# A kernel's order of issue worked out by a list schedule and pinned, in place of the framework's own scheduler

## The chip, the cores and the metric

One core of a Trainium2 chip (trn2) runs the whole program. The metric is the device time of one execution in microseconds, the median of several runs. The engines are named PE or TensorE (matmuls and transposes), ACT or ScalarE, DVE or VectorE, POOL or GpSimd, and SP, whose queue issues the weight transfers.

## The reference

Two layers, each a half-step SwiGLU feed-forward net, a token mixer, and another half-step net, each between RMS norms. 256 tokens, width 1024, feed-forward width 2816, float32.

```python
for l in range(DEPTH):
    g = norm_g[l]
    h = swiglu_ffn(rmsnorm(x, g[0]), ffn_w_gate[l, 0], ffn_w_up[l, 0], ffn_w_down[l, 0])
    x = x + 0.5 * rmsnorm(h, g[1])
    h = hybrid_mixer(rmsnorm(x, g[2]), w_in[l], ..., w_out[l])
    x = x + rmsnorm(h, g[3])
    h = swiglu_ffn(rmsnorm(x, g[4]), ffn_w_gate[l, 1], ffn_w_up[l, 1], ffn_w_down[l, 1])
    x = x + 0.5 * rmsnorm(h, g[5])
```

`swiglu_ffn` is `(silu(h @ w_gate) * (h @ w_up)) @ w_down`. `hybrid_mixer` projects `h` by `w_in` into the inputs of three groups and multiplies their joined outputs by `w_out`: gated linear attention over chunks of 64 tokens (4 heads), a causal depthwise convolution of width 31 over 256 channels with layer norm and swish, and attention in a window of 128 tokens with 8 query heads, ALiBi and a sink per head.

## The kernel before

The 256 tokens are two tiles t of 128. Activations lie transposed as the stationary operand, weights stream past. A float32 product is made of three matmuls in the type fp32r (`mm3`, L183 to L186): each operand is split into a rounded `hi` and a rest `lo`. For the weights this is the work of `emit_unit` (L153): one DMA by SP into one of 4 `raw` buffers (L160), the cast `hi` on ScalarE (L164), the subtraction `lo` on VectorE (L170) or, for some of the mixer's units, GpSimd, each into one of 8 buffers. `done` releases a buffer once both token tiles have used it and emits the next unit.

A feed-forward net (`ffn`) goes over seven chunks of its 2816 columns, 384 or 512 wide: gate matmuls (into PSUM tiles `gu`), silu on ScalarE, up matmuls, the product `h` on VectorE, its transposes (L328), and the down matmuls of the chunk before (into `ga` and `sa`). `pre` (L262) makes a net's input: the norm's sum of squares (L259), transposes of `x` (L271), scaled evictions `xh` on ScalarE (L275) and the rest `xl` on VectorE (L279). It needs `gT`, the transposed norm weights (L190, L191). `post` (L285) is the norm of an output tile, added to `x`.

`late_setup` runs behind the gate matmuls of the second chunk of the first net: it loads constants over ScalarE's DMA queue. `tb` (L217) is loaded into one of two buffers `sc`, GpSimd makes the ALiBi table from it by eight operations (L219) and masks (L220), and only then has `ts` (L225) and after it `cwr`, the 31 + 1 rows of conv weights and bias (L228, L229), a buffer. TensorE transposes `cwr` (L235).

The mixer's pieces stand in a string (`SCRIPT`, L125): projections c, k, q, b, a of each tile, then queries and scores (S), their output (O), the gates (G, R), the linear attention (K, L, P, C), conv taps (T), the conv's end (Y, Z), the output projection (W) and the norm with the next net's input (A). A tap takes a product on ScalarE and a sum on GpSimd (L641, L642), or one operation on VectorE (L635). `kv_in` evicts the keys (`ts`, L680) for transposes (L685). `swa_q` evicts the queries (`sq`, L692), TensorE transposes them (L695), ScalarE evicts again (`qp`, L697). `swa_scores` makes scores (L711, L715), the sink's term (L718, L719), the negated maximum (L720) and the exponentials (L723), which `swa_out` transposes (L735) and multiplies with the values (L745).

The text of the program is not the order of issue. The framework's scheduler takes the traced instructions and, with its own cost model and the program's order as priority, sets each engine's order. `tc.issue_after` tells it not to put the setup and the mixer ahead of a named instruction.

Of the kernel before, what the change touches and what calls it, by code (L numbers as in the profile page):

```python
# [1 line left out]

# [12 lines left out]
PSUM = bass.MemoryType.PSUM  # L15
# [32 lines left out]
def trunk_kernel(  # L48
# [5 lines left out]
    nc = tc.nc  # L54
    V, G, A, PE = nc.vector, nc.gpsimd, nc.scalar, nc.tensor
# [10 lines left out]
    def nm(s):  # L66
        uid[0] += 1
        return f"{s}_{uid[0]}"
# [82 lines left out]
    state = {"emitted": 0, "released": 0, "m": 0}  # L151
# [47 lines left out]
    one = cp.tile([P, 1], F32, tag="one", name="one")  # L199
# [6 lines left out]
    def bcast(dst, src):  # L206
        A.dma_start(out=dst, in_=src.partition_broadcast(P))

    def late_setup():
# [52 lines left out]
    def pre(t, l, n):  # L262
        x = xs[t]
        r = rstd_of(sumsq([x[:, 0:512], x[:, 512:1024]])) if (t, l, n) != (0, 0, 0) else None
        hi = [ap.tile([P, P], F32R, tag=f"xh{t}_{k}", name=nm("xh")) for k in range(KT)]
        lo = [ap.tile([P, P], F32R, tag=f"xl{t}_{k}", name=nm("xl")) for k in range(KT)]
        for hf in range(2):
            ps = ps_tile("tr")
            for i in range(4):
                k = hf * 4 + i  # L270
                PE.transpose(out=ps[:, i * P:(i + 1) * P], in_=x[:, k * P:(k + 1) * P], identity=ident)  # L271
            for i in range(4):
                k = hf * 4 + i
# [137 lines left out]
        A.activation(out=out, in_=out, func=AF.Exp, scale=-1.0)  # L411

    def mixer(l, first, xT, after):
        with tc.issue_after(state["silu"].ins):
            ld = A.preload_act_table_set("natural_log_exp_and_others")
        with tc.issue_after(ld.ins):
            return mixer_body(l, first, xT, after)

    def mixer_body(l, first, xT, after):
        gng = mp.tile([P, 256], F32, tag="gng", name=nm("gng"))  # L420
        bcast(gng, gng_d[l].rearrange("h d -> (h d)"))
        lng = mp.tile([P, 256], F32, tag="lng", name=nm("lng"))
        bcast(lng, lng_d[l])
        lnb = mp.tile([P, 256], F32, tag="lnb", name=nm("lnb"))
        bcast(lnb, lnb_d[l])
        nr = {}

        def neg(t):
# [414 lines left out]
    xT[1]()  # L843


_INS = ['x', 'norm_g', 'ffn_w_gate', 'ffn_w_up', 'ffn_w_down', 'w_in', 'gla_w_gate2', 'gla_b_gate', 'gla_norm_g',
# [52 lines left out]
```

## Time and profile before

| what | value |
|---|---|
| median of 3 runs | 1011.09 us (1008.58 to 1011.55) |
| the profiled execution | 1012.63 us, its span 1010.6 us |
| mean granted clock of TensorE | 0.986 |
| TensorE busy | 969.1 us, 96% |
| VectorE, ScalarE, GpSimd busy | 592.4, 543.6, 133.9 us |
| read from memory | 169.88 MB, 169 GB/s over the span |

The page gives averages over the span. The stages differ: the four feed-forward nets, and the two mixers between them at about 206 to 330 and 696 to 822 us. So the views below are taken by stage. A granted clock of 1.00 is 2.4 GHz, one of 0.50 is 1.2 GHz. Idle time in brackets is that of the engine just before the row.

### The profile page before, as it was taken

Reading aid. Unit: us, or ns where it says so; the run is one execution under the profiler, and the core shown is the slowest. Engines: PE = TensorE matmul, PEld = TensorE weight load, DVE = VectorE, ACT = ScalarE, POOL = GpSimd, SP = SyncE. Lnnn points to the kernel's source line nnn. Section 1 sums busy time; section 2 is a strip of 40 time slices with the busy share of each in tenths; the row PEclk is TensorE's granted clock in tenths of the full one; section 3 lists DMA queues with packets and bytes.
Section 4 is the critical chain, followed back from the end, with each engine's and each line's share of the span. In section 5 each row is a group of like instructions: output and inputs, shape, how many; then the busy total and the mean of one; then the engine's idle time right before and its main releaser. Section 6 shows DMA issues by size and latency. Waiting matters only on the chain.

```text
span 1010.6 us, 13078 instructions
## 1 busy us (share of the span) xinstructions
PE 969.1 (96%) x4745; PEld 825.8 (82%) x4745; DVE 592.4 (59%) x894; ACT 543.6 (54%) x935; POOL 133.9 (13%) x158
## 2 busy tenths in 40 slices
PE   7959999998899999999999999999899999999997
PEld 7848888987688988888998888898787888888896
DVE  6634554567787764554576554456576886554453
ACT  7524443577885654443475444455778575444441
POOL 1110000027551000000000000000576110000000
PEclk9979999999999999999999999999989999999999
DMA  8846655734143676655648666564522348666541
GB/s 292 281 119 187 188 177 159 211 115 149 63 131 105 222 230 188 187 177 164 185 141 270 188 187 193 158 201 139 183 83 101 94 142 270 188 187 194 156 150 42
DMA packets 81971, 171.78 MB, mean 170 GB/s; under 512 B 5939, under 2 KB 29682, under 8 KB 81907
## 3 DMA queue, kind: packets, MB, share of 16 engines
q1 hardware_dynamic: 79952, 168.97, 53.9%
q10 hardware_dynamic: 1955, 1.98, 0.8%
q8 instruction: 37, 0.61, 0.2%
q14 instruction: 27, 0.22, 0.1%
HBM read 169.88 MB, written 1.05 MB: 169 GB/s over the span
## 4 chain that ended last, share of the span: by engine, by line
PE 79%; ACT 7%; DVE 4%; DMA 3%; POOL 3%; issue 2%; POOLq 0%; SPq 0%; ACTq 0%; DVEq 0%
PE gu L185 16%; PE gu L186 16%; PE gu L184 16%; PE ga L184 4%; PE ga L185 4%; PE ga L186 4%; PE sa L186 4%; PE sa L185 4%; PE sa L184 4%; PE tr L328 2%; ACT hi L164 2%; DVE lo L170 1%; ACT sc L723 1%; POOL cy L642 1%; DMA raw<-in_ffn_w_gate_dram 1%
## 5 line engine op out<-in xcount | busy, mean ns | idle before, releaser
L170 DVE TENSOR_TENSOR lo<-raw,hi 128x1024 fp32r<-128x1024 f32 (+3 forms) x316 | 369.4, 1174 | 309.2 <-ACT hi L164 308.3
L164 ACT CAST hi<-raw 128x1024 fp32r<-128x1024 f32 (+2 forms) x336 | 331.7, 995 | 371.9 <-PE gu L186 206.9
L185 PE MATMUL gu<-lo,xh 128*128 128x512 f32 (+2 forms) x864 | 326.1, 377 | 0.0
L184 PE MATMUL gu<-hi,xh 128*128 128x512 f32 (+2 forms) x864 | 326.0, 377 | 0.1
L186 PE MATMUL gu<-hi,xl 128*128 128x512 f32 (+2 forms) x864 | 324.8, 376 | 0.0
L185 PEld LDWEIGHTS gu<-lo,xh 128*128 128x128 f32 x864 | 163.7, 190 | 23.4 <-DVE lo L170 0.8
L184 PEld LDWEIGHTS gu<-hi,xh 128*128 128x128 f32 x864 | 163.6, 189 | 22.8 <-ACT sg L315 0.4
L186 PEld LDWEIGHTS gu<-hi,xl 128*128 128x128 f32 x864 | 163.8, 190 | 22.5
L252 POOL TENSOR_TENSOR rstd<-var,mhalf 128x1 f32<-128x1 f32 x24 | 13.1, 547 | 744.5 <-DVE var L251 744.5
L184 PE MATMUL ga<-hi,hh 128*128 128x512 f32 x176 | 69.4, 394 | 0.0
L185 PE MATMUL ga<-lo,hh 128*128 128x512 f32 x176 | 69.0, 392 | 0.0
L186 PE MATMUL ga<-hi,hl 128*128 128x512 f32 x176 | 68.9, 392 | 0.0
L186 PE MATMUL sa<-hi,hl 128*128 128x512 f32 x176 | 68.9, 391 | 0.0
L184 PE MATMUL sa<-hi,hh 128*128 128x512 f32 x176 | 68.8, 391 | 0.0
L185 PE MATMUL sa<-lo,hh 128*128 128x512 f32 x176 | 68.5, 389 | 0.0
L170 POOL TENSOR_TENSOR lo<-raw,hi 128x1024 fp32r<-128x1024 f32 (+1 forms) x20 | 47.0, 2354 | 34.8 <-ACT hi L164 34.8
L642 POOL TENSOR_TENSOR cy<-tc,cy 128x256 f32<-128x256 f32 x60 | 43.9, 732 | 15.4 <-ACT tc L641 11.7
L186 PEld LDWEIGHTS ga<-hi,hl 128*128 128x128 f32 x176 | 33.3, 189 | 7.1
L185 PEld LDWEIGHTS ga<-lo,hh 128*128 128x128 f32 x176 | 33.3, 189 | 6.6
L184 PEld LDWEIGHTS ga<-hi,hh 128*128 128x128 f32 x176 | 33.3, 189 | 6.6
L184 PEld LDWEIGHTS sa<-hi,hh 128*128 128x128 f32 x176 | 33.1, 188 | 6.9
L185 PEld LDWEIGHTS sa<-lo,hh 128*128 128x128 f32 x176 | 33.1, 188 | 6.9
(186 smaller groups left out, 997.7 us busy)
## 6 DMA issues: line engine op xcount, KB each, us to landing
raw<-in_ffn_w_down_dram SPq DMA_DIRECT2D x88, 512.0 KB, 3.4
raw<-in_ffn_w_gate_dram SPq DMA_DIRECT2D x64, 512.0 KB, 3.7
raw<-in_ffn_w_up_dram SPq DMA_DIRECT2D x64, 512.0 KB, 3.8
raw<-in_ffn_w_gate_dram SPq DMA_DIRECT2D x32, 384.0 KB, 3.3
raw<-in_ffn_w_up_dram SPq DMA_DIRECT2D x32, 384.0 KB, 3.3
raw<-in_w_in_dram SPq DMA_DIRECT2D x16, 512.0 KB, 5.5
raw<-in_w_out_dram SPq DMA_DIRECT2D x16, 512.0 KB, 3.8
raw<-in_w_in_dram SPq DMA_DIRECT2D x16, 392.0 KB, 3.9
```

The lines of the kernel that those rows point to most:

```text
L164: A.copy(out=hi[:, :n], in_=raw[:, :n])
L170: eng.tensor_tensor(out=lo[:, :n], in0=raw[:, :n], in1=hi[:, :n].bitcast(F32), op=ALU.subtract)
L184: PE.matmul(out=out, lhsT=xh, rhs=wh, start=start, stop=False)
L185: PE.matmul(out=out, lhsT=xh, rhs=wl, start=False, stop=False)
L186: PE.matmul(out=out, lhsT=xl, rhs=wh, start=False, stop=stop)
L252: G.tensor_tensor(out=r, in0=v, in1=mhalf[:, 0:1], op=ALU.pow)
L328: PE.transpose(out=ps[:, i * P:(i + 1) * P], in_=h[:, i * P:(i + 1) * P], identity=ident)
L642: G.tensor_tensor(out=yc, in0=m, in1=yc, op=ALU.add)
L723: A.activation(out=sc[:, h, :], in_=sc[:, h, :], func=AF.Exp, bias=mx[:, h:h + 1], accum_out=ls[:, h:h + 1])
```

## The change

No instruction is added, dropped or altered. When all instructions have been traced, `arrange` (new) gives each a cost, simulates the engines, and takes the instruction that can start first, the earlier one of the program at a tie. The order found is pinned on each engine by dependences without semaphores, and so is the order in which buffers are opened by different engines. The mixer's three broadcasts of norm weights, and the setup, keep their place behind a named instruction by `issue_after`, now the program's own.

```diff
+    held = []
+    @contextmanager
+    def issue_after(ins):
+        ...
     def late_setup():
-        with tc.issue_after(state["silu"].ins):
+        with issue_after(state["silu"].ins):
             late_setup_body()
...
     xT[1]()
+    arrange(tc, held)
...
+class Op:
+    def cost(self):
+        ...
+        if self.dma:
+            self.busy, self.after = (.37 if e == "SP" else .45), None
+        ...
+        elif e == "DVE":
+            ...
+                t = (.205 if op == "ISA" else .145) + .00105 * max(n, 1)
+        elif e == "Pool":
+            ...
+                t = .25 + .0019 * n if n > 8 else (.55 if n == 1 else 1.04)
+def order_of_issue(ops):
+    ...
+    for _ in range(n):
+        for e in engs:
+            if e not in known:
+                c = None
+                for k in ready[e]:
+                    when = room(ops[k])
+                    if when is None:
+                        continue
+                    when = max(when, free[e], at[k])
+                    if c is None or when < c[0] - 1e-9:
+                        c = (when, k)
+                        ...
+                known[e] = c
+        start, k = min(c for c in known.values() if c is not None)
+        o = ops[k]
+        end = start + (o.after or 0.)
+        if o.dma:
+            landed = end = max(start + 3.5, landed + o.bytes / 390e3)
+        ...
+def arrange(tc, held):
+    ...
+    out, first = order_of_issue(ops)
+    info = mybir.DependencyInfo(mybir.DependencyClass.NoSync, mybir.DependencyReason.DATA)
+    for e in ("PE", "Activation", "DVE", "Pool", "SP"):
+        for a, b in zip(out[e], out[e][1:]):
+            tc.add_manual_dep(b.i, a.i.name, info, reason="order of issue")
+    for b, a in first:
+        if a.eng != b.eng:
+            tc.add_manual_dep(b.i, a.i.name, info, reason="order of buffers")
```

By the new functions every line of the kernel from L209 on stands 7 or 8 lines further down.

**Place 1, the setup.** ScalarE, from the first cast behind the first DMAs of the setup, before (`hi` and `raw` are buffers of one weight unit):

```order
L164 CAST hi_552<-raw_551 128x1024
L164 CAST hi_572<-raw_571 128x1024
L225 DMA ts_522<-in_constants_dram 128x576
L228 DMA cwr<-in_conv_w_dram 31x2x256
L229 DMA cwr<-in_conv_b_dram 1x512
L164 CAST hi_590<-raw_589 128x1024
L164 CAST hi_608<-raw_607 128x1024
L164 CAST hi_626<-raw_625 128x1024
L164 CAST hi_648<-raw_647 128x1024
```

and now:

```order
L164 CAST hi_552<-raw_551 128x1024
L164 CAST hi_572<-raw_571 128x1024
L164 CAST hi_590<-raw_589 128x1024
L233 DMA ts_522<-in_constants_dram 128x576
L164 CAST hi_608<-raw_607 128x1024
L164 CAST hi_626<-raw_625 128x1024
L236 DMA cwr<-in_conv_w_dram 31x2x256
L237 DMA cwr<-in_conv_b_dram 1x512
L164 CAST hi_648<-raw_647 128x1024
```

The second `ts` DMA stands behind one more cast, the two `cwr` DMAs behind three more. TensorE at the transposes of `cwr`, in the middle of the up matmuls (`gu`) of the second chunk, before:

```order
L186 MATMUL gu_557<-hi_440,xl_112 128x512
L184 MATMUL gu_557<-hi_440,xh_105 128x512
L235 MATMUL tr_529<-cst,cwr 128x32 x4
L185 MATMUL gu_557<-lo_441,xh_105 128x512
L186 MATMUL gu_557<-hi_440,xl_113 128x512
```

and now, at the end of the first half of the down matmuls of the first chunk:

```order
L184 MATMUL sa_201<-hi_476,hh_421 128x512
L185 MATMUL sa_201<-lo_477,hh_421 128x512
L243 MATMUL tr_529<-cst,cwr 128x32 x4
L186 MATMUL sa_201<-hi_476,hl_422 128x512
L336 MATMUL tr_671<-cst,h_631 128x128 x4
L336 MATMUL tr_680<-cst,h_633 128x128 x4
```

Between the two places lie 31 matmuls. In the first microseconds, the copy of `gT` (L191) now stands behind the first two `lo` subtractions on VectorE, and a second weight cast and a sum of squares stand ahead of the first `xh` evictions on ScalarE.

**Place 2, mixer 1 on ScalarE, the queries of the second tile** (`sq_2250`, evicted from `gu_2201`; `tc` are conv taps, `sc` the exponentials of the first tile's scores), before:

```order
L641 ACTIVATE tc_2283<-upad,cwT 128x256
L641 ACTIVATE tc_2287<-upad,cwT 128x256
L719 ACTIVATE es_2151<-es_2151 128x4
L723 ACTIVATE sc_2141,ls_2155<-sc_2141,mx_2142 128x128 x4
L719 ACTIVATE es_2173<-es_2173 128x4
L164 CAST hi_2245<-raw_2244 128x784
L723 ACTIVATE sc_2163,ls_2177<-sc_2163,mx_2164 128x128 x4
L692 ACTIVATE sq_2250<-gu_2201,rstd_1869 128x512
L641 ACTIVATE tc_2291<-upad,cwT 128x256
```

and now:

```order
L648 ACTIVATE tc_2279<-upad,cwT 128x256
L699 ACTIVATE sq_2250<-gu_2201,rstd_1869 128x512
L164 CAST hi_2233<-raw_2232 128x784
L726 ACTIVATE es_2151<-es_2151 128x4
L730 ACTIVATE sc_2141,ls_2155<-sc_2141,mx_2142 128x128 x4
L726 ACTIVATE es_2173<-es_2173 128x4
L164 CAST hi_2245<-raw_2244 128x784
L730 ACTIVATE sc_2163,ls_2177<-sc_2163,mx_2164 128x128 x4
L704 ACTIVATE qp_2257<-sa_2252 128x512
```

The eviction has gone ahead of two casts (`hi_2233`, `hi_2245`) and of all exponentials.

**Place 3, mixer 1 on TensorE, the transposes of the same queries** (`sa_2252`; `sa_2259` are those of the exponentials; `gu_2669` is projection a, `ga_2361` projection b), before, four matmuls into projection a of the first tile:

```order
L184 MATMUL gu_2669<-hi_2209,xh_1689 128x392
L185 MATMUL gu_2669<-lo_2210,xh_1689 128x392
L186 MATMUL gu_2669<-hi_2209,xl_1697 128x392
L184 MATMUL gu_2669<-hi_2209,xh_1690 128x392
L695 MATMUL sa_2252<-cst,sq_2250 128x128 x4
L735 MATMUL sa_2259<-cst,sc_2141 128x128 x4
L185 MATMUL gu_2669<-lo_2210,xh_1690 128x392
L186 MATMUL gu_2669<-hi_2209,xl_1698 128x392
```

and now, in projection b of the first tile:

```order
L184 MATMUL ga_2361<-hi_2058,xh_1690 128x392
L185 MATMUL ga_2361<-lo_2059,xh_1690 128x392
L186 MATMUL ga_2361<-hi_2058,xl_1698 128x392
L184 MATMUL ga_2361<-hi_2070,xh_1691 128x392
L702 MATMUL sa_2252<-cst,sq_2250 128x128 x4
L185 MATMUL ga_2361<-lo_2071,xh_1691 128x392
L742 MATMUL sa_2259<-cst,sc_2141 128x128
L186 MATMUL ga_2361<-hi_2070,xl_1699 128x392
L742 MATMUL sa_2259<-cst,sc_2141 128x128
L184 MATMUL ga_2361<-hi_2070,xh_1692 128x392
L185 MATMUL ga_2361<-lo_2071,xh_1692 128x392
L742 MATMUL sa_2259<-cst,sc_2141 128x128
```

Both sets of transposes stand some 20 matmuls earlier, those of the exponentials one by one between projection matmuls. In the same way in each mixer the conv gate's last steps go ahead of a weight cast and of the key eviction `ts` on ScalarE, output matmuls (W) are spread earlier, and six fewer of them stand between the last matmul of the first output tile and the transposes of `x` behind its norm (L271).

## Rows read from the trace of the kernel before

**Rows 1.** The page, busy time, share of the span and instructions of each engine.

```profile
PE 969.1 (96%) x4745; PEld 825.8 (82%) x4745; DVE 592.4 (59%) x894; ACT 543.6 (54%) x935; POOL 133.9 (13%) x158
```

**Rows 2.** Six stretches of the span. Columns: the stretch and its length, busy time (and instructions) of PE, PEld, DVE, ACT and POOL, the mean granted clock of TensorE, the mean busy share of the DMA engines, GB/s.

```profile
0.00:10.00 10.00, 4.30 (x15) 3.48 (x16) 3.02 (x10) 6.32 (x16) 3.55 (x12) 1.00 0.83 275
50.00:63.00 13.00, 2.51 (x13) 1.84 (x12) 2.74 (x4) 1.99 (x2) 4.65 (x6) 0.69 0.35 92
63.00:206.00 143.00, 143.00 (x661) 121.33 (x662) 73.00 (x75) 62.47 (x73) 0.57 (x1) 0.98 0.59 176
226.00:240.00 14.00, 11.99 (x67) 9.99 (x66) 8.84 (x9) 10.41 (x20) 8.86 (x7) 1.00 0.63 201
240.00:260.00 20.00, 15.33 (x74) 13.39 (x73) 17.51 (x46) 16.27 (x45) 14.59 (x16) 0.91 0.35 127
708.00:820.00 112.00, 103.42 (x559) 86.92 (x558) 80.83 (x194) 82.94 (x207) 56.34 (x58) 0.97 0.36 114
```

**Rows 3.** The waits of TensorE: the tile and line that stood, what released it, us in total, times, the longest.

```profile
PE tr L235 <- DMA cwr<-in_conv_b_dram: 10.5, 1, 10.5
PE sa L695 <- ACT sq L692: 8.5, 4, 2.5
PE sa L685 <- ACT ts L680: 3.7, 2, 2.0
PE ga L453 <- DVE tg L616: 1.9, 2, 1.0
```

**Rows 4.** The chain of work that ended last, 40 to 64 us: start, length, what.

```profile
55.60 6.52 DMA cwr<-in_conv_b_dram
```

**Rows 5.** The timeline of TensorE, 48 to 75 us: start, length, line, operation and tiles, and in brackets the idle time before it with what ended it. Between the first two rows here stand 15 more matmuls of the same kind.

```profile
47.75 0.39 PE L186 MATMUL gu<-hi,xl 128*128 128x512 f32 x1
...
51.38 0.39 PE L184 MATMUL gu<-hi,xh 128*128 128x512 f32 x1
62.26 0.60 PE L235 MATMUL tr<-cst,cwr 32*128 32x32 f32 x4 [10.49 <-DMA cwr<-in_conv_b_dram]
...
72.84 1.03 PE L328 MATMUL tr<-cst,h 128*128 128x128 f32 x8
```

**Rows 6.** Four stretches, cut at the records of the granted clock; columns as in rows 2.

```profile
54.85:68.51 13.66, 6.25 (x18) 4.96 (x19) 5.21 (x7) 3.04 (x3) 0.00 (x0) 0.50 0.38 104
256.24:259.65 3.41, 3.32 (x13) 3.32 (x14) 3.04 (x9) 2.99 (x9) 1.46 (x2) 0.50 0.49 159
734.11:737.52 3.41, 3.41 (x9) 2.67 (x8) 0.93 (x6) 2.70 (x5) 3.17 (x5) 0.50 0.00 0
747.76:751.17 3.41, 3.41 (x16) 3.41 (x14) 2.04 (x5) 3.30 (x10) 2.27 (x4) 0.50 0.25 99
```

**Rows 7.** The timelines of ScalarE, VectorE and TensorE in the first 13 us, one after the other.

```profile
7.15 2.16 ACT L275 ACTIVATE xh<-tr,gT 128x128 fp32r<-128x128 f32 x8
...
6.32 0.25 DVE L191 COPY gT<-tr 128x96 f32<-128x96 f32 x1
7.28 0.96 DVE L170 TENSOR_TENSOR lo<-raw,hi 128x768 fp32r<-128x768 f32 x1 [0.71 <-ACT hi L164]
...
7.57 0.69 PE L184 MATMUL gu<-hi,xh 128*128 128x384 f32 x1
```

**Rows 8.** The timeline of ScalarE in mixer 1.

```profile
232.15 0.84 ACT L164 CAST hi<-raw 128x784 fp32r<-128x784 f32 x1 [0.75 <-DMA raw<-in_w_in_dram]
...
233.22 0.46 ACT L680 ACTIVATE ts<-ga,rstd 128x256 f32<-128x256 f32 x1
...
255.61 0.66 ACT L692 ACTIVATE sq<-gu,rstd 128x512 f32<-128x512 f32 x1
```

**Rows 9.** The timeline of TensorE around the transposes of L695, in mixer 1 and (the last two rows) in mixer 2.

```profile
243.22 0.66 PE L695 MATMUL sa<-cst,sq 128*128 128x128 f32 x4 [2.19 <-ACT sq L692]
243.63 0.48 PE L186 MATMUL gu<-hi,xl 128*128 128x512 f32 x1
...
244.18 0.39 PE L185 MATMUL gu<-lo,xh 128*128 128x512 f32 x1
...
248.48 0.39 PE L186 MATMUL gu<-hi,xl 128*128 128x512 f32 x1
...
256.33 1.11 PE L695 MATMUL sa<-cst,sq 128*128 128x128 f32 x4 [2.48 <-ACT sq L692]
...
733.18 0.66 PE L695 MATMUL sa<-cst,sq 128*128 128x128 f32 x4 [1.99 <-ACT sq L692]
...
747.03 0.66 PE L695 MATMUL sa<-cst,sq 128*128 128x128 f32 x4 [1.86 <-ACT sq L692]
```

**Rows 10.** VectorE's and GpSimd's timelines at 247 us, and the group of all operations of L718 (count, busy time, mean ns of one).

```profile
247.95 1.84 DVE L718 TENSOR_TENSOR es<-snk,mx 128x4 f32<-128x4 f32 x1
...
247.15 4.45 POOL L170 TENSOR_TENSOR lo<-raw,hi 128x784 fp32r<-128x784 f32 x2
...
L718 DVE TENSOR_TENSOR es<-snk,mx 128x4 f32<-128x4 f32 x8 | 6.1, 757 | 0.1
```

**Rows 11.** The timeline of TensorE at the end of mixer 1.

```profile
319.84 0.39 PE L186 MATMUL gu<-hi,ol 128*128 128x512 f32 x1
...
323.74 1.03 PE L271 MATMUL tr<-cst,x 128*128 128x128 f32 x8
```

**Rows 12.** The page, DMA issues: KB each, median us from issue to landing.

```profile
raw<-in_w_in_dram SPq DMA_DIRECT2D x16, 512.0 KB, 5.5
```

More of the change, by code (lines that the diff above doesn't have):

```diff
@@ L207, in bcast @@
         A.dma_start(out=dst, in_=src.partition_broadcast(P))
+    held = []
+    @contextmanager
+    def issue_after(ins):
+        old = len(nc.cur_bb.bb.instructions)
+        yield
+        held.extend((i.name, ins.name) for i in list(nc.cur_bb.bb.instructions)[old:] if i.engine == ins.engine)
     def late_setup():
-        with tc.issue_after(state["silu"].ins):
+        with issue_after(state["silu"].ins):
             late_setup_body()
@@ L413, in mixer, with mixer_body @@
     def mixer(l, first, xT, after):
[L414 to L419, printed above, removed]
+        ld = A.preload_act_table_set("natural_log_exp_and_others")
+        return mixer_body(l, first, xT, after, ld)
+    def mixer_body(l, first, xT, after, ld):
         gng = mp.tile([P, 256], F32, tag="gng", name=nm("gng"))
[L421 removed]
         lng = mp.tile([P, 256], F32, tag="lng", name=nm("lng"))
[L423 removed]
         lnb = mp.tile([P, 256], F32, tag="lnb", name=nm("lnb"))
[L425 removed]
+        with issue_after(ld.ins):
+            bcast(gng, gng_d[l].rearrange("h d -> (h d)"))
+            bcast(lng, lng_d[l])
+            bcast(lnb, lnb_d[l])
         nr = {}
@@ L843, in trunk_kernel, with __init__, meets, holds @@
     xT[1]()
+    arrange(tc, held)
+LAT = {("PE", "Activation"): .04, ("PE", "DVE"): .04, ("DVE", "PE"): .055, ("Activation", "PE"): .055,
+       ("DMA", "PE"): .06, ("DVE", "Pool"): .08, ("Activation", "Pool"): .08, ("DMA", "Pool"): .08}
+PIPE = .165
+class Acc:
+    def __init__(self, a):
+        b = a.bass_ap
+        t = b.tensor
+        self.tile = t if type(t).__name__ == "Tile" else None
+        self.pat = [tuple(q) for q in b.ap]
+        self.n = 1
+        for _, q in self.pat[1:]:
+            self.n *= q
+        self.bytes = self.pat[0][1] * self.n * 4
+        if self.tile is None:
+            return
+        row = 1
+        for q in t.shape[1:]:
+            row *= q
+        self.r = "float32r" in str(b.dtype)
+        self.psum = "PSUM" in str(t.space)
+        self.p0, self.c0 = b.offset // row, b.offset % row
+        self.p1 = self.p0 + self.pat[0][1]
+        self.c1 = self.c0 + 1 + sum((q - 1) * s for s, q in self.pat[1:])
+    def meets(self, o):
+        return self.p0 < o.p1 and o.p0 < self.p1 and self.c0 < o.c1 and o.c0 < self.c1
+    def holds(self, o):
+        return self.p0 <= o.p0 and self.p1 >= o.p1 and self.c0 <= o.c0 and self.c1 >= o.c1
@@ new lines, in order_of_issue, with room @@
+def order_of_issue(ops):
+    seen, psum_last = {}, {}
+    tables = dict(kind=None, load=None, now=[], before=[])
+    tile, tags = {}, {}
+    for o in ops:
+        for a in o.r:
+            for p, b, wr in seen.get(a.tile.name, ()):
+                if wr and p is not o and a.meets(b):
+                    o.pre[p.k] = True
+        for a in o.w:
+            for p, b, wr in seen.get(a.tile.name, ()):
+                if p is not o and a.meets(b):
+                    o.pre[p.k] = True
+        for a in o.w:
+            h = [x for x in seen.get(a.tile.name, ()) if not a.holds(x[1])]
+            seen[a.tile.name] = h + [(o, a, True)]
+        for a in o.r:
+            seen.setdefault(a.tile.name, []).append((o, a, False))
+        if o.eng == "PE":
+            t = o.w[0].tile.name
+            if t in psum_last:
+                o.pre.setdefault(psum_last[t].k, False)
+            psum_last[t] = o
+        if o.op == "LoadActFuncSet":
+            for p in tables["now"]:
+                o.pre.setdefault(p.k, False)
+            tables["load"] = o
+        kind = "s" if o.func == "Silu" else "e" if o.func in ("Exp", "Ln") else None
+        if kind:
+            if kind != tables["kind"]:
+                tables.update(kind=kind, before=tables["now"], now=[])
+            for p in tables["before"] + ([tables["load"]] if tables["load"] else []):
+                o.pre.setdefault(p.k, False)
+            tables["now"].append(o)
+        for a in o.r + o.w:
+            t = a.tile
+            if t.name not in tile:
+                own = tags.setdefault(t.tag, dict(slots=[None] * t.tag_meta.bufs, next=0, n=0))
+                tile[t.name] = dict(tag=own, i=own["n"], left=0, end=0., slot=None)
+                own["n"] += 1
+            if t.name not in o.tiles:
+                o.tiles.append(t.name)
+                tile[t.name]["left"] += 1
+    n = len(ops)
+    post = [[] for _ in ops]
+    wait = [len(o.pre) for o in ops]
+    for o in ops:
+        for p, data in o.pre.items():
+            post[p].append((o.k, data))
+    engs = ("PE", "Activation", "DVE", "Pool", "SP", "X")
+    ready = {e: [] for e in engs}
+    for o in ops:
+        if not wait[o.k]:
+            ready[o.eng].append(o.k)
+    at, free, out, known = [0.] * n, dict.fromkeys(engs, 0.), {e: [] for e in engs}, {}
+    landed = 0.
+    first = []
+    def room(o):
+        when = 0.
+        for name in o.tiles:
+            t = tile[name]
+            if t["slot"] is not None:
+                continue
+            tag = t["tag"]
+            if t["i"] != tag["next"]:
+                return None
+            f = [0. if s is None else tile[s]["end"] + .05 for s in tag["slots"] if s is None or not tile[s]["left"]]
+            if not f:
+                return None
+            when = max(when, min(f))
+        return when
+    for _ in range(n):
[5 more added lines that the diff above has]
+                    if when is None:
+                        continue
+                    when = max(when, free[e], at[k])
+                    if c is None or when < c[0] - 1e-9:
+                        c = (when, k)
+                        if when <= free[e] + 1e-9:
+                            break
+                known[e] = c
[4 more added lines that the diff above has]
+            landed = end = max(start + 3.5, landed + o.bytes / 390e3)
+        free[o.eng] = start + o.busy
+        out[o.eng].append(o)
+        ready[o.eng].remove(k)
+        dirty = {o.eng}
+        for name in o.tiles:
+            t = tile[name]
+            tag = t["tag"]
+            if t["slot"] is None:
+                _, t["slot"] = min((0. if s is None else tile[s]["end"], j) for j, s in enumerate(tag["slots"])
+                                   if s is None or not tile[s]["left"])
+                tag["slots"][t["slot"]] = name
+                if tag["next"]:
+                    first.append((o, tag["opened"]))
+                tag["opened"] = o
+                tag["next"] += 1
+                dirty.update(engs)
+            t["left"] -= 1
+            t["end"] = max(t["end"], end)
+            if not t["left"]:
+                dirty.update(engs)
+        for q, data in post[k]:
+            p = ops[q]
+            if p.eng == o.eng == "PE" or not data:
+                r = start + (o.busy if p.eng == o.eng else 0.)
+            else:
+                r = end + (.03 if p.eng == o.eng and not o.dma else LAT.get(("DMA" if o.dma else o.eng, p.eng), .04))
+            at[q] = max(at[q], r)
+            wait[q] -= 1
+            if not wait[q]:
+                l = ready[p.eng]
+                j = len(l)
+                while j and l[j - 1] > q:
+                    j -= 1
+                l.insert(j, q)
+                dirty.add(p.eng)
+        for e in dirty:
+            known.pop(e, None)
+    return out, first
@@ new lines, in arrange @@
+def arrange(tc, held):
+    ops = [Op(k, i) for k, i in enumerate(tc.nc.cur_bb.bb.instructions)]
+    index = {o.i.name: o for o in ops}
+    for late, early in held:
+        index[late].pre.setdefault(index[early].k, False)
+    out, first = order_of_issue(ops)
[6 more added lines that the diff above has]
+            tc.add_manual_dep(b.i, a.i.name, info, reason="order of buffers")
```

65 lines of the change are left out of this document (64 added, 1 removed).

## The prediction

> **What bounds the kernel now.** Read the busy shares first: TensorE is busy 96% of the span [rows 1]. So only what TensorE loses can be won, 1010.6 - 969.1 = 41.5 us of idle time and whatever it runs slowly. The stretches say where it loses [rows 2]: nothing in the feed-forward bodies (143.00 of 143 us busy), 5.7 us in the first 10, 10.5 us in one hole at 50 to 63, 2.0 and 4.7 us in the first 34 us of mixer 1, and 8.6 us in mixer 2. The waits name the work that TensorE stood for [rows 3]: the transposes of the conv weights `cwr` (10.5), four transposes of the query eviction (L695, 8.5), two of the key eviction (L685, 3.7). The granted clock gives the rest [rows 6]: after the hole it is at 0.50, 1.2 GHz, until 68.51, and there are three more such stretches of 3.41 us, each close behind a stall. Work at half the clock costs half its busy time: 6.25/2 = 3.1 us behind the hole, 3.41/2 = 1.7 in each of the others. An order of issue can give back these things alone; it adds and drops no instruction.
>
> The profiled execution (1012.63 us) is 1.5 above the median of the runs shown. The sum is made against it, and 1.5 is taken off at the end. A difference within 0.3%, 3 us, is what a measurement of this kernel can't tell from none.
>
> **Part 1: start and setup, likely to gain about 6.**
>
> *Start.* The eight scaled evictions `xh` on ScalarE began at 7.15, right after the copy of `gT` on VectorE (6.32, 0.25 us) [rows 7]. In the new order that copy stands behind two `lo` subtractions of 0.96 us, so 1.9 us later, and a second cast goes ahead of `xh`. TensorE's first projection (7.57) follows `xh`. I take a delay of 1.9 us at the end of the first chunk.
>
> *The hole.* TensorE stopped after its matmul at 51.38 and reached the `cwr` transposes at 62.26, when the DMA issued at 55.60 had landed (6.52 us) [rows 4, 5]. In the new order 31 matmuls of the next pieces stand ahead of those transposes. Their pitch is 0.227 us (16 steps from 47.75 to 51.38 [rows 5]), so TensorE gets there 31 x 0.227 = 7.0 us later, plus the 1.9 of the start: 51.8 + 7.0 + 1.9 = 60.7. On ScalarE the `ts` issue now has one cast more ahead of it and the `cwr` issues have three more. If the casts are not held up they delay `cwr` by 2 to 3 us, and the start may add up to 1.9; if they only take ScalarE's idle time of before, nothing. I take 2, the middle: landing at 64.1, a stall of 3.4 us. Then 0.6 us of transposes, 64.8, and a low-clock stretch like the three shorter ones, 1.7 us. Before, the same 31 matmuls were through when the transposes of L328 began at 72.84 [rows 5]. Gain: 72.9 - 64.8 - 1.7 = 6.4.
>
> Its bounds: a landing at 62.1 as before and no low clock give 72.9 - 62.9 = 10; a landing at 68 (the stream of weights now keeps running past it, and shares the engines with it), with a low clock that costs 3.1, gives 72.9 - 68.7 - 3.1 = 1.
>
> Before, the weight stream stood still in the hole: 92 GB/s against 176 in the feed-forward body [rows 2]. The Trainium skill (DMA: Bandwidth & Descriptors, "Why a DMA increments its semaphore by 16 and not by 1" and "Queues, rings and completion order") says that a transfer is spread over the largest count of engines that divides its two slowest dimensions, and that each engine takes turns between its queues by packet. The 31 rows of `conv_w` would then sit on one engine and share it with the weights; by that rule the landing goes to the late bound, not the early one. No stretch of this trace has both at once.
>
> **Part 2: the mixers, gain about 3 and 4.** In both layers the moves are the same.
>
> - *L685 (2.0 us in mixer 1, 1.7 in mixer 2).* The eviction `ts` (233.22) stood behind a cast that waited for its weights until 232.15 [rows 8]. Now that cast is behind it, and TensorE comes one matmul later. What remains is the way through the conv gate, which is pulled ahead of `ts`. I take 0.5 left in each: 1.5 and 1.2.
> - *L695, first (2.19; 1.99) [rows 9].* TensorE comes five rows later, with three more matmuls (0.7 us) ahead after earlier shifts; the eviction is not earlier by much. I take 0.9 from each.
> - *L695, second (2.48; 1.86) [rows 9].* The query eviction `sq` came at 255.61, behind all eight exponentials of the scores, while the matmuls that make its input had ended at 248.9 [rows 8, 9]. Now it stands ahead of them. But TensorE is also moved: its transposes of `sq`, and those of the exponentials `sc` with them, stand some 20 matmuls earlier, spread one or two matmuls apart, which is just the time the plan gives each exponential. Whoever is late there is seen at once. The 2.48 goes; I put 1.0 us of new stall in its place. Reason: the small operation L718 takes 757 ns on average and 1.84 us where it ran beside GpSimd's `lo` [rows 10], while the plan's formula gives it 0.145 + 0.00105 x 4 = 0.15. That is 0.6 late, and L720 behind it is of the same kind.
> - *Low clock.* Stretch at 256.24 goes with the stall: 1.7. Both in mixer 2 (734.11, 747.76): 3.4.
> - *Small waits*: L453 (1.9 in both by the waits [rows 3]) and others like it, 0.4 from each mixer.
> - *New stall at the end.* The normalisation between the last output tile and the transposes of `x` takes from 320.23 to 323.74, 3.5 us [rows 11]. Before, TensorE filled it with twelve matmuls of the other tile; now six of them have gone earlier. 6 x 0.227 = 1.4 stay as cover: loss 3.5 - 1.4 = 2.1. At most 3.5, at least 0.7.
> - *More switches.* The new order spreads projection matmuls among fp32 ones: 98 changes of kind for 84, that is 7 more returns. The first matmul after a return shows 0.48 us, the next ones 0.39 [rows 9]. 7 x 0.09 = 0.6; with the changes the other way some 1.0.
>
> Mixer 1: 1.5 + 0.9 + (2.48 - 1.0) + 1.7 + 0.4 - 2.1 - 1.0 = 2.9. Mixer 2: 1.2 + 0.9 + (1.86 - 1.0) + 3.4 + 0.4 - 2.1 - 1.0 = 3.7. Bounds: if every stall and low clock goes and no new one comes, mixer 2 gains 8.6 + 3.4 = 12 and mixer 1, whose moves and waits are the same with one low stretch fewer, 11; if each old stall only makes way for another, nothing, or a loss (rival 3).
>
> The feed-forward bodies count for nothing: their TensorE has no idle time to give, and the trace shows its other engines at about half (73.0 and 62.5 of 143 us) [rows 2], which covers their shifts. The tail after the last matmul is not moved.
>
> **Sum.** 1012.6 - 6.4 - 2.9 - 3.7 = 999.6; less 1.5, **998 us**.
>
> **Rivals.**
>
> 1. *Only the setup pays.* For it: in mixer 1 ScalarE is busy 16.27 of 20 us and VectorE 17.51 [rows 2], so a stall taken away at one tile comes back at the next. Against it: 1.7 us a stretch of low clock need no faster engine. 1011.1 - 6.4 = 1004.7.
> 2. *`cwr` slips to the late bound.* TensorE still stands there; the setup gives 1. 1011.1 - 1 - 6.6 = 1003.5. If both rivals hold, about 1010.
> 3. *Slower: the pinned queues block at their head.* An engine issues in order, and the order now rests on fixed prices. Every `w_in` transfer is priced at 3.5 us or its place in a line at 390 GB/s. The trace shows 5.5 us as their median [rows 12]; where a cast stands at ScalarE's head and its weights come 2.0 us later than planned, the taps, exponentials and evictions behind it wait, and TensorE for them. With 8 such casts exposed of the 32 `w_in` units of both mixers, 8 x 2.0 = 16 us, the gain of 13 is gone; with 16 exposed, 32 us, it is 1011.1 - 13 + 32 = 1030. Against it: before, that is how the first L685 stall arose, so the old order suffers from it too, and units are issued up to eight ahead.
>    The same holds for VectorE beside GpSimd: the Trainium skill (SBUF — State Buffer, "Who interferes with whom") has a VectorE operation with two SBUF inputs and a GpSimd one that reads SBUF lock each other out for a whole instruction, and no cost of the plan knows it. The trace agrees at 247.95: 1.84 us beside `lo`.
> 4. *No change in effect*, the freed time being eaten by the start and the new stall at the end: 1009 to 1013.
>
> **How the numbers follow.** Forecast 0.60 (990 to 1003), rival 1 alone 0.13, rival 2 alone 0.12, rivals 3 and 4: 0.07 each. The missing 0.01 and more of the low side is a schedule that wins nearly all, 1011.1 - 10 - 23 = 978. Range: the forecast with its better half of the mixer bounds, down to **987**, and up over rivals 1 and 2 to **1008**. Faster by over 0.3%: 0.60 + 0.13 + 0.12 and a little of the rest, **0.87**; within 0.3%: **0.06**; slower: **0.07**.
>
> **What would show it.** Waits of TensorE: the `cwr` line falls from 10.5 to 3 or 4 us at about 61; L685 (now L692) nearly gone; L695 (L702) under half of 8.5; transposes of `sc` (L742) new with 1 us a mixer; transposes of `x` (L279) new with some 2 us each. Granted clock: no low stretch of 13 us, one of about 3.4 behind `cwr`, none at the query transposes. First projection matmul at 9.5, not 7.57. I am wrong if the `cwr` wait stays above 8, if the low stretches in the mixers stay, or if ScalarE shows casts in the mixer that wait for DMA with TensorE idle behind them.

## The result: slower, by 1.3%

The changed kernel takes 1024.02 us (median of 4 runs, 1022.27 to 1025.79) where the kernel before takes 1010.88. The ratio is 1.0134, with a 95% interval of 1.0105 to 1.0163. The profiled execution took 1022.27 us, its span is 1020.5 us, 9.9 longer than before. What follows splits these 9.9 us; the medians lie 13.1 apart, since two of the changed kernel's four runs have a granted clock of 0.988 in place of 0.992 and take 3.4 us more. The forecast was 998, with 987 to 1008 as its range.

The page of the changed kernel, busy time first: TensorE does the same work (970.1 us, [rows 1] had 969.1), and stands idle 9 us more.

```profile
PE 970.1 (95%) x4745; PEld 825.7 (81%) x4745; DVE 593.3 (58%) x894; ACT 543.5 (53%) x935; POOL 145.5 (14%) x158
```

The waits of TensorE (tile and line, what released it, us in total, times, longest), without the wait for the first load that both kernels have (6.0 us here, 5.7 before), to be set against [rows 3]:

```profile
PE tr L279 <- DVE x L302: 5.6, 6, 3.4
PE gu L186 <- DVE xl L287: 5.4, 2, 2.9
PE tr L243 <- DMA cwr<-in_conv_b_dram: 4.0, 1, 4.0
PE tr L485 <- DVE tc L482: 3.9, 4, 1.1
PE sa L460 <- DVE ts L755: 3.0, 4, 0.9
PE ga L460 <- DVE tg L623: 3.0, 2, 1.5
...
PE sa L702 <- ACT sq L699: 0.9, 2, 0.5
```

The reader sees what was aimed at: `cwr` fell from 10.5 to 4.0 us, the query transposes (now L702) from 8.5 to 0.9, the key transposes are off the list. In their place stand the transposes of `x` (L279), the matmuls with `xl` (L186), and many waits of about 1 us in the mixers.

Where the time went is read from a mark that both kernels have. The silu of a chunk (L315, now L323) stands at a fixed place of TensorE's work, so the difference of its starts, meaned over the two token tiles, is what was won or lost so far. In the last chunk of the first net it started at 181.82 and 183.86 us before, and now at:

```profile
176.70 0.58 ACT L323 ACTIVATE sg<-gu,rstd 128x384 f32<-128x384 f32 x1
177.74 0.58 ACT L323 ACTIVATE sg<-gu,rstd 128x384 f32<-128x384 f32 x1 [0.46 <-PE gu L186]
```

That is 5.1 and 6.1 us earlier, 5.6 in the mean. The same reading at four places, in us against the kernel before, minus is earlier (the last column is the span's end):

| kernel | end of net 1 | net 2, behind mixer 1 | net 3 | net 4, behind mixer 2 | end |
|---|---|---|---|---|---|
| the change | -5.6 | -1.3 | +4.1 | +8.8 | +9.9 |
| difference to the column ahead | -5.6 | +4.3 | +5.4 | +4.7 | +1.1 |

Within the four nets nothing is lost (behind the first two chunks the mark stays still from chunk to chunk). The setup paid as forecast. Each mixer lost 4 to 5, the seam between nets 2 and 3, which the prediction had not looked at, 5.4, and the tail 1.1.

The seam before, VectorE's timeline. The four `lo` subtractions ran ahead of the norm's sum `var` and of both products `y`, and TensorE did not stand:

```profile
514.16 3.68 DVE L170 TENSOR_TENSOR lo<-raw,hi 128x768 fp32r<-128x768 f32 x4
517.76 0.21 DVE L251 TENSOR_SCALAR var<-ss 128x1 f32<-128x1 f32 x1
517.88 1.28 DVE L290 TENSOR_TENSOR y<-sa,gpost 128x512 f32<-128x512 f32 x2
```

And in the changed kernel:

```profile
512.74 0.86 DVE L287 SCALAR_TENSOR_TENSOR xl<-tr,gT,xh 128x128 fp32r<-128x128 f32 x3
516.37 0.69 DVE L298 TENSOR_TENSOR y<-sa,gpost 128x512 f32<-128x512 f32 x1 [2.77 <-ACT junk L267]
516.98 0.60 DVE L287 SCALAR_TENSOR_TENSOR xl<-tr,gT,xh 128x128 fp32r<-128x128 f32 x2
517.50 3.55 DVE L170 TENSOR_TENSOR lo<-raw,hi 128x768 fp32r<-128x768 f32 x4
520.97 0.68 DVE L298 TENSOR_TENSOR y<-sa,gpost 128x512 f32<-128x512 f32 x1
521.57 0.20 DVE L259 TENSOR_SCALAR var<-ss 128x1 f32<-128x1 f32 x1
522.42 1.41 DVE L302 SCALAR_TENSOR_TENSOR x<-y,rstd,x 128x512 f32<-128x512 f32 x2 [0.65 <-POOL rstd L260]
```

VectorE's product `y` (L298) stands at the head from 513.60 on and waits 2.77 us for ScalarE's sum of squares over the same PSUM tile. ScalarE's timeline has four casts ahead of that sum:

```profile
512.67 3.08 ACT L164 CAST hi<-raw 128x768 fp32r<-128x768 f32 x4
515.60 0.65 ACT L267 ACTIVATE junk<-sa 128x512 f32<-128x512 f32 x1
```

The four `lo` subtractions of these casts could start from 513.6 on, but can't pass `y`. They run from 517.50 to 521.05, and only then come the second `y`, the norm's sum and the update of `x`. The chain of waits of the same stretch (start, length, what) has all of it:

```profile
515.75 0.60 ACT junk L267 x2
516.98 0.60 DVE xl L287 x2
517.58 3.47 DVE lo L170 x4
521.05 0.60 DVE y L298
521.85 0.55 POOL rstd L260
522.42 0.76 DVE x L302
523.23 1.12 PE tr L279 x4
```

TensorE stands for 3.45 us there (last row), and the same sort of wait comes at the first projection behind a mixer (third row); the first row is `cwr`, the second the end of mixer 1:

```profile
65.45 0.54 PE L243 MATMUL tr<-cst,cwr 32*128 32x32 f32 x4 [4.03 <-DMA cwr<-in_conv_b_dram]
...
316.41 0.41 PE L460 MATMUL ga<-cst,tg 128*128 128x128 f32 x2 [1.48 <-DVE tg L623]
...
326.29 0.44 PE L186 MATMUL gu<-hi,xl 128*128 128x384 f32 x1 [2.57 <-DVE xl L287]
...
523.23 1.12 PE L279 MATMUL tr<-cst,x 128*128 128x128 f32 x4 [3.45 <-DVE x L302]
```

Apart from the stretch at the span's end, which every kernel here has, there are four stretches of low clock. Three of them are new ones, behind the new waits. They are (columns as in [rows 2]) of 3.41 us each, so 1.7 us lost in each, as in [rows 6]:

```profile
65.54:68.95 3.41, 3.41 (x15) 3.07 (x16) 1.85 (x3) 2.02 (x3) 0.00 (x0) 0.50 0.86 285
318.13:321.54 3.41, 3.41 (x14) 2.83 (x13) 0.93 (x2) 1.84 (x6) 0.00 (x0) 0.50 0.00 0
522.93:526.34 3.41, 3.11 (x13) 3.04 (x14) 1.08 (x3) 2.68 (x10) 0.00 (x0) 0.50 1.03 382
826.71:830.13 3.42, 3.42 (x13) 3.42 (x12) 2.82 (x6) 0.00 (x0) 0.52 (x1) 0.50 0.43 116
```

### The profile page after: what moved, and what is told of

It is laid out like the page before. It is cut to its first block, busy times and chain, and to the rows that moved or that the text cites. A ratio compares the mean times of both kernels' runs of the same rounds, so it can differ in the third digit from the quotient of the medians.

```text
span 1020.5 us, 13105 instructions
## 1 busy us (share of the span) xinstructions
PE 970.1 (95%) x4745; PEld 825.7 (81%) x4745; DVE 593.3 (58%) x894; ACT 543.5 (53%) x935; POOL 145.5 (14%) x158
## 4 chain that ended last, share of the span: by engine, by line
PE 75%; DVE 7%; ACT 7%; issue 4%; POOL 3%; DMA 2%; SPq 0%; ACTq 0%; DVEq 0%; POOLq 0%
PE gu L186 16%; PE gu L184 16%; PE gu L185 15%; PE ga L186 4%; PE ga L185 4%; PE ga L184 4%; PE sa L186 3%; PE sa L184 3%; PE sa L185 3%; PE tr L336 2%; DVE lo L170 2%; ACT hi L164 1%; ACT xh L283 1%; ACT junk L267 1%; DVE xl L287 1%
## 5 line engine op out<-in xcount | busy, mean ns | idle before, releaser
L170 DVE TENSOR_TENSOR lo<-raw,hi 128x1024 fp32r<-128x1024 f32 (+3 forms) x316 | 374.7, 1192 | 313.4 <-ACT hi L164 312.9
L186 PE MATMUL gu<-hi,xl 128*128 128x512 f32 (+2 forms) x864 | 324.6, 376 | 5.5 <-DVE xl L287 5.4
L186 PEld LDWEIGHTS gu<-hi,xl 128*128 128x128 f32 x864 | 163.5, 189 | 29.9 <-DVE xl L287 6.8
L186 PE MATMUL sa<-hi,hl 128*128 128x512 f32 x176 | 69.0, 392 | 0.0
L186 PE MATMUL ga<-hi,hl 128*128 128x512 f32 x176 | 68.7, 390 | 0.0
L170 POOL TENSOR_TENSOR lo<-raw,hi 128x1024 fp32r<-128x1024 f32 (+1 forms) x20 | 49.7, 2496 | 22.8 <-ACT hi L164 22.8
L649 POOL TENSOR_TENSOR cy<-tc,cy 128x256 f32<-128x256 f32 x60 | 47.5, 791 | 14.9 <-ACT tc L648 11.5
L323 ACT ACTIVATE sg<-gu,rstd 128x512 f32<-128x512 f32 (+1 forms) x48 | 31.3, 653 | 17.6 <-PE gu L186 15.5
L287 DVE SCALAR_TENSOR_TENSOR xl<-tr,gT,xh 128x128 fp32r<-128x128 f32 x96 | 27.3, 344 | 20.0 <-ACT xh L283 20.0
L186 PEld LDWEIGHTS ga<-hi,hl 128*128 128x128 f32 x176 | 33.0, 188 | 7.0
L186 PEld LDWEIGHTS sa<-hi,hl 128*128 128x128 f32 x176 | 33.1, 188 | 6.8
```

The lines of the kernel that those rows point to most:

```text
L170: eng.tensor_tensor(out=lo[:, :n], in0=raw[:, :n], in1=hi[:, :n].bitcast(F32), op=ALU.subtract)
L186: PE.matmul(out=out, lhsT=xl, rhs=wh, start=False, stop=stop)
L323: state["silu"] = A.activation(out=sg[:, :w], in_=pg_[:, :w], func=AF.Silu, scale=r)
L649: G.tensor_tensor(out=yc, in0=m, in1=yc, op=ALU.add)
```

## The experiments

The reading behind the experiments: the list schedule knows what a reader waits for, the last writer, but it has no edge between two readers. The built program does have one: where two engines read the same PSUM tile, the later one in the program waits on a semaphore for the earlier. So the plan lets `y` start beside the sum of squares, puts it early, and the pinned queue then stands behind it. The rival reading: a greedy order has no slack, and whatever rules it knows it loses to what it does not price.

**read_order: the rule added to the plan.**

```diff
         for a in o.r:
+            if a.psum:
+                for p, b, wr in seen.get(a.tile.name, ()):
+                    if not wr and p.eng != o.eng:
+                        o.pre[p.k] = True
+        for a in o.r:
             seen.setdefault(a.tile.name, []).append((o, a, False))
```

> The change with one rule added to its plan: a reader of a PSUM tile waits for earlier readers (in the program's order) on other engines, as the y products of L298 do behind the sums of squares of L267 in the trace. Theory (the plan's missing rule causes the loss): the stall of 3.45 us before the transposes of x between the two neighbouring feed-forward nets goes with what is behind it (5.4 us), the one before the first projection after each mixer (2.6 and 2.9 us) too, the tail gets 1 us shorter: 1020.5 - 5.4 - 1.0 - 5.4 = about 1009 us of span, 1 to 3 us under the kernel before. Rival (a greedy order without slack loses whatever its rules, or contention between engines does it): the new stalls move elsewhere, 1017 us or more.

Measured: 1001.37 us, ratio 0.9913 (0.988 to 0.9946), span 999.5. With five lines more the same plan is 23 us faster than the change. The same seam on VectorE:

```profile
503.62 2.16 DVE L287 SCALAR_TENSOR_TENSOR xl<-tr,gT,xh 128x128 fp32r<-128x128 f32 x8 [0.56 <-ACT xh L283]
505.69 3.55 DVE L170 TENSOR_TENSOR lo<-raw,hi 128x768 fp32r<-128x768 f32 x4
509.17 0.21 DVE L259 TENSOR_SCALAR var<-ss 128x1 f32<-128x1 f32 x1
509.29 1.28 DVE L298 TENSOR_TENSOR y<-sa,gpost 128x512 f32<-128x512 f32 x2
```

The four `lo` now stand ahead, at 505.69, in the time in which VectorE idled; the norm follows, and TensorE's waits for `x` and `xl` are off the list:

```profile
PE tr L243 <- DMA cwr<-in_conv_b_dram: 4.5, 1, 4.5
PE sa L460 <- DVE ts L755: 3.0, 4, 0.9
PE tr L279 <- DVE gT L191: 2.9, 1, 2.9
PE tr L485 <- DVE tc L482: 2.3, 2, 1.2
PE ga L460 <- DVE tg L623: 2.0, 2, 1.0
```

The theory held and the rival fell. The gain is nearly twice what I had expected (21.0 us of span for some 11.5): the waits in the middle of the mixers shrank too (L485 from 3.9 to 2.3, L460 behind `tg` from 3.0 to 2.0), and the low stretches at the end of both mixers went with them. One stretch of 3.41 us came in mixer 2, at 738.50, which is why that mixer gains less (table below).

A further rival is that any new order would have mended the mixers. Against it speak the eight wholly pinned plans of the table below: the five with the rule, whole or in part, gain 1.1 to 4.0 us in each mixer, the three without it lose 3.2 to 6.3. Which of the added edges does it in the mixers was not taken apart.

**read_order_post: the rule for the tiles of a norm alone.** The same edit, with `and p.func == "Square"` in the condition.

> The same rule for the tiles alone that a sum of squares has read (post's y behind junk), not for the transposes that pre evicts (xl behind xh). Theory that post alone matters: the same time as with the whole rule, about 1009 us. Rival (the evictions of pre matter as well): 2 us or more slower than with the whole rule, with waits of TensorE for xl.

Measured: 1004.21 us, ratio 0.9941 (0.9922 to 0.996). The wait for `xl` is still there, but at 0.6 us; `y` behind the sum of squares is nearly the whole. By its time alone, 2.8 us slower than with the whole rule, the rival held. By stage the answer is: post matters most, and the rest of the rule is worth some 1 us in each mixer (table below); the setup, where the two orders of `cwr` are alike, differs by 1.4 by itself.

**one_move: one instruction moved.** On the changed kernel's own order.

```diff
     out, first = order_of_issue(ops)
+    d = out["DVE"]
+    at = lambda n: next(i for i, o in enumerate(d) if o.w and o.w[0].tile.name.startswith(n))
+    y = d.pop(at("y_1136_"))
+    d.insert(at("lo_1123_") + 1, y)
```

> The changed kernel with one instruction moved on one engine: the first y product of the second token tile between the two feed-forward nets stands behind the four lo subtractions, where the plan with the rule puts it, not ahead of them. Theory (a head of queue that waits for a PSUM reader holds the four lo, and these then hold the norm): the 3.45 us stall before the transposes of x and the low clock behind it go, 5.4 us in that stretch and nothing elsewhere; span about 1015 us. Rival (the stretch is slow because the engines are full there): under 1.5 us.

Measured: 1019.32 us, ratio 1.0094 (1.0076 to 1.0113), against 1.0134. The seam costs 1.4 us now in place of 5.4 (table), so the single `y` was 4.0, its low stretch included. Of the 1.4 left 0.6 can be seen: at the first token tile a `y` still stands between the sum of squares and `var`. VectorE in that stretch; the first row is that `y`:

```profile
509.16 0.69 DVE L298 TENSOR_TENSOR y<-ga,gpost 128x512 f32<-128x512 f32 x1 [1.41 <-ACT junk L267]
...
516.17 3.55 DVE L170 TENSOR_TENSOR lo<-raw,hi 128x768 fp32r<-128x768 f32 x4
519.64 0.68 DVE L298 TENSOR_TENSOR y<-sa,gpost 128x512 f32<-128x512 f32 x1
```

The mixers, where nothing was moved, lose 4.3 and 3.2, for 4.3 and 4.7; the low stretch at 827 is not in this execution, and that is worth 1.7. So the place of one waiting instruction in one queue carried 4 us, and the rival, under 1.5, fell. Net 1, where nothing was moved either, gains 3.5 in place of 5.6: by 2.1 us that stage differs from one execution to another.

**setup_only: the first net alone pinned.** The plan (with the rule) orders the instructions up to the first mixer; everything behind them is left to the framework's scheduler, with `tc.issue_after` as before.

```diff
+        mine = [o for o in out[e] if o.k < end]
-        for a, b in zip(out[e], out[e][1:]):
+        for a, b in zip(mine, mine[1:]):
```

> Only the instructions of the first feed-forward net (with the late setup) are pinned to the plan's order; everything behind them is ordered by the framework's scheduler as before. Theory (the gain of 5.6 us seen at the second chunk's end is real and independent of the rest): 1011 - 5.6 = 1005.4 us, wait for cwr 4.0 us. Rival (the earlier arrival is given back, since the mixer's start is bound by something else): 1009 us or more.

Measured: 1007.41 us, ratio 0.9972 (0.9949 to 0.9995). It pays, though the interval ends close to 1, and 2 to 3 us in place of 5.6. The waits of TensorE (L706 and L696 are the L695 and L685 of before, and stand as in [rows 3]):

```profile
PE sa L706 <- ACT sq L703: 8.4, 4, 2.5
...
PE tr L243 <- DMA cwr<-in_conv_b_dram: 5.3, 1, 5.3
PE sa L696 <- ACT ts L691: 4.0, 2, 2.2
PE tr L279 <- DVE gT L191: 2.6, 1, 2.6
```

What is won at the end of the first net (2.5) is not given back (table), so the rival fell. The rest is the setup's own spread: the wait for `cwr` was 4.0, 4.5, 5.2, 5.2 and 5.3 us in five kernels that order it in the same way (the change, read_order, read_order_post, one_move and this one), and the low clock behind it lasted 3.41 us in three of them and 6.83 in the other two.

**read_order_dma: ScalarE's transfers priced by the trace.**

```diff
         if o.dma:
-            landed = end = max(start + 3.5, landed + o.bytes / 390e3)
+            if o.eng == "SP":
+                landed = end = max(start + 3.5, landed + o.bytes / 390e3)
+            else:
+                end = start + 4.3
```

and the first table load, at no cost, no longer holds the transfers issued behind it.

> The rule, and the prices of ScalarE's DMAs mended: they no longer stand in one line with the weight transfers (landing 4.3 us after the issue, as the trace shows for grow) and the first table load no longer holds them. The copy of gT then stands first on VectorE. Theory (the start's delay comes from that price): the stall of 2.6 us before the first transposes goes and the whole is 2 us faster than with the rule alone. Rival (the start is absorbed by the wait for cwr): the wait for cwr grows by as much, no difference.

Measured: 997.04 us, ratio 0.9872 (0.9828 to 0.9915), 4 us faster than the rule alone. The wait of 2.6 to 2.9 us for `gT` is gone, as expected, and the wait for `cwr` falls too, to 3.1, with no low stretch behind it. The reason for the late `gT` was the price: the small transfer of the norm weights stood in the plan's one line behind those of `x` and of the first weight units.

**dma_only: the same prices without the rule.**

> The mended prices of ScalarE's DMAs without the PSUM rule. Theory (the two errors of the plan add up): the start and the setup gain some 4 us over the change, the stalls behind the y products stay, about 1018 to 1020 us. Rival (any small mend of the plan shuffles the order, and the gain of the first runs was luck): the mixers and the stretch between the nets move by several us as well.

Measured: 1026.27 us, ratio 1.0159 (1.0144 to 1.0174). My theory that the two errors add up fell: the stalls behind `y` stay, as expected, but the start gains nothing.

```profile
PE gu L186 <- DVE xl L287: 5.8, 2, 2.9
...
PE tr L279 <- DVE x L302: 5.6, 6, 3.4
...
PE gu L185 <- DVE lo L170: 3.7, 3, 2.3
```

TensorE now waits there for `lo` (3.7 us in all, with a low stretch at 20.18 to 23.59). The `cwr` wait did fall to 3.0, and the wait for `gT` went. VectorE's queue shows what came in their place: it stood 1.31 and 1.90 us at an `xl` whose `xh` on ScalarE was late, with `lo` behind it. That the missing rule set this order (`xh` and `xl` read the same PSUM tile) is argued, not shown. The rival, a mere shuffle, is not borne out: the waits of the mixers and of the seam are those of the change, and the +2.0 and -1.5 us by which the mixers differ from it (table) are about the 1.7 of one low stretch, one more in mixer 1 and one fewer in mixer 2.

**cwr_price: `cwr` priced at 6.5 us.** On read_order_dma.

```diff
-                end = start + 4.3
+                end = start + (6.5 if o.w and o.w[0].tile.name.startswith("cwr") else 4.3)
```

> Rule and mended DMA prices, and the transfer of cwr priced at the 6.5 us that every trace shows (6.3 to 6.8) in place of 4.3. TensorE's transposes of cwr then stand ten rows further down. Theory (the wait of 3.1 to 5.3 us for cwr is the plan's price error): the wait falls under 1.5 us, 2 to 3 us faster than without it, about 994.5 us. Rival (cwr's landing slips along, or the next consumer stands instead): no difference.

Measured: 993.08 us, ratio 0.9834 (0.9818 to 0.985), the fastest of all. The wait for `cwr` fell to 0.4 us (the transposes stand ten rows later), and, as in read_order_dma, there is no low stretch before the end of the span:

```profile
PE tr L243 <- DMA cwr<-in_conv_b_dram: 0.4, 1, 0.4
```

The gain over read_order_dma, 1 to 4 us, has overlapping ends; that the wait all but went is plain.

**port_lock: VectorE and GpSimd exclude each other in the plan.** On read_order_dma: an operation of VectorE with two SBUF tensors starts no earlier than the last GpSimd operation that reads SBUF ends, and the other way.

> Rule and mended DMA prices, and in the plan a VectorE operation with two SBUF tensors and a GpSimd operation that reads SBUF exclude each other for their whole length (the trace shows 1.8 us for a 0.16 us operation beside GpSimd). Theory (what is left in the mixers, some 5 us each, comes from such collisions, which the plan doesn't price): 2 to 6 us faster than without, 991 to 995 us. Rival (the lock is not that strict, and a plan that is too pessimistic idles engines): no gain or a loss of up to 5 us.

Measured: 1000.5 us, ratio 0.9906 (0.9887 to 0.9924), 3.5 us slower than without, though the ends of the two just overlap (998.11 and 998.83). By its time the rival held, by its reason only in part. The collisions did go: the operation of [rows 10] (now L725; shortest, median and longest in ns) without the exclusion in the plan, and with it:

```profile
L725 DVE TENSOR_TENSOR es<-snk,mx x8: 267/557/1831, 236.6 to 745.0; 128x4 f32<-128x4 f32 x8
...
L725 DVE TENSOR_TENSOR es<-snk,mx x8: 148/159/1143, 242.3 to 752.3; 128x4 f32<-128x4 f32 x8
```

VectorE was busy 584.4 us in place of 593.3, and TensorE's idle time in the two mixers, from the last chunk of the net before to the first of the net behind, is the same (15.4 and 15.6 us in all). The waits only stand at other places (L576 behind `kk`, 3.7 in all). What was lost there is clock: 13.7 us at 0.50, from 301.37, 782.64 and 792.88 on, where read_order_dma has none. TensorE was busy 299.3 us in these two stretches for 294.1, and the two mixers lose 5.0 against read_order_dma (table). Why equal idle time brought low clock in one kernel and none in the other was not taken further.

The runs by stage, read as in the first table:

| kernel | net 1 | mixer 1 | seam | mixer 2 | tail | span |
|---|---|---|---|---|---|---|
| the change | -5.6 | +4.3 | +5.4 | +4.7 | +1.1 | +9.9 |
| one_move | -3.5 | +4.3 | +1.4 | +3.2 | +1.1 | +6.5 |
| dma_only | -2.3 | +6.3 | +5.5 | +3.2 | +1.1 | +13.8 |
| read_order_post | -3.7 | -2.6 | +0.2 | -1.2 | +0.5 | -6.8 |
| read_order | -5.1 | -3.8 | -0.3 | -2.4 | +0.5 | -11.1 |
| read_order_dma | -9.1 | -3.8 | -0.3 | -4.0 | +0.5 | -16.7 |
| cwr_price | -10.2 | -3.8 | -0.3 | -4.0 | +0.5 | -17.8 |
| port_lock | -8.2 | -1.1 | -0.3 | -1.7 | +0.5 | -10.8 |
| setup_only | -2.5 | +0.4 | 0.0 | +0.1 | 0.0 | -2.0 |

## Why the prediction was wrong

**The step that failed** is that every term was costed as if the plan knew every wait of the program. It knew none between two readers of one PSUM tile. Two terms rest on that belief. The first is the list of new stalls in part 2: the mixers were to gain 2.9 and 3.7 and lost 4.3 and 4.7, which is 15.6 of the 22.9 us by which the stages missed the forecast. The second is the sentence that the nets count for nothing, that the other engines at half load cover their shifts, and that the tail is not moved: 5.4 and 1.1 of the 22.9 (the setup has the other 0.8). That sentence is true of the bodies: the mark stays still there. It left out the seams, where post's norm is a chain over ScalarE, VectorE and GpSimd that TensorE waits for, and there the order of VectorE was not laid beside the one before. The half load was that of a body, too. At the seam VectorE, the third busy time of this row (columns as in [rows 2]), had little room before the change:

```profile
508.00:520.24 12.24, 12.15 (x65) 10.76 (x64) 11.25 (x23) 9.35 (x23) 1.62 (x3) 1.00 0.44 143
```

With the missing rule alone put in, the seam is 5.7 us shorter and the mixers 8.1 and 7.1, which turns their loss into a gain; the tail is 0.6 shorter (in the change its last `y` stands between the sum of squares and `var`; the other 0.5 every wholly pinned kernel has, and its cause stays open). At the seam a single moved instruction shows the cause. In the mixers it is shown for the rule as a whole.

The Trainium skill (PSUM — Partial Sum Buffer, "Terms") says that two engines may not touch one PSUM bank at once, reads against reads included. The trace agrees in its order: ScalarE's sum over that tile ran from 515.60 to 516.25 and `y` began at 516.37. The prediction drew on the skill for rules that change a duration, and not for this one, which adds a wait.

**Point by point.**

- *Start*: 1.9 us of delay forecast at the end of the first chunk; 3.1 at the first mark and 1.7 at the second. Right in size, though the row was not: TensorE waited 2.59 us in the middle of the transposes, for the buffer that `gT` held.
- *Hole*: a landing at 64.1, a wait of 3.4 and a low stretch of 3.4 us were forecast; TensorE began at 65.45 after 4.03, and the low stretch is 3.41. Gain 5.6 against 6.4. Right. Rival 2, a late landing, did not come: from issue to landing it took 6.36 us, with 136 GB/s moved meanwhile, and 6.52 before [rows 4], with 63.
- *L685, L695*: 1.2 to 1.5, 0.9 and the whole of the second were forecast to go. All went but 0.9 in total. But the key's wait had moved to the conv gate (L485, 3.9 in all), where I had put 0.5 a mixer.
- *Low clock*: all three old stretches went, as forecast, and three new ones came.
- *End of a mixer*: 2.1 us of new stall forecast before the transposes of `x`. It came as 1.48 us at L460 and 0.46 behind it, where 0.97 was before, with a low stretch. Right in kind.
- *The sum for the kernel that I thought I was costing*: with the rule, the stages are -5.1, -3.8, -0.3 and -2.4, where I had -6.4, -2.9, 0 and -3.7. The stalls that were to go did go there, but that the sums of the mixers come so close is in part luck: TensorE did not wait for `x` at the end of a mixer, where 2.1 us each were forecast, and waits that the forecast doesn't name stand in their place (L460 behind `ts`, 3.0 in all).
- *Rival 3* had the right mechanism, a pinned queue that blocks at its head, and 0.07 as its chance. It had the wrong head: it looked for casts that wait for transfers and for collisions. TensorE's waits name no cast, and pricing the collisions (port_lock) did not pay. None of the prediction's own signs of being wrong looks at VectorE's queue.

## What to carry to other kernels

When an order is computed and pinned, compare what the plan waits for with what the built program waits for, engine by engine, before any price: here the one missing edge cost 23 us and each mended price won some 4 at most, since the instruction that waits takes its whole queue with it. Cost the seams where one stage's norm feeds the next, by the order of every engine on that chain, and not only the stages that show idle time before. A kernel's gain that sits in one stage can be read early: take a mark that both kernels have and follow its difference through the span.

## What the runs showed of the hardware

- The conv weights and bias, 31 + 1 rows, take 6.3 to 6.8 us from the second issue to the landing in all ten kernels, in the kernel before with 63 GB/s moved meanwhile and in the changed one with 136.
- The operation of [rows 10], 128x4 on VectorE, took 0.80 us in the mean of 8 in the changed kernel, 0.15 by its plan. The Trainium skill (SBUF — State Buffer, "Who interferes with whom") has a VectorE instruction with two SBUF inputs and a GpSimd one that reads SBUF contend for a port that one of them holds for its whole instruction. The trace agrees: the plan that keeps the two apart (port_lock) brought the median of this operation from 557 to 159 ns. It came out 3.5 us slower all the same, by its low clock.
